# The front half of a transformer block on one core: instructions recorded, list-scheduled by the kernel itself, and held in that order on every engine

## The chip, the core and the metric

The kernel runs on one core of a Trainium2 chip. A core has five engines with a queue of instructions each: TensorE (PE in the profile; its weight loads are PEld), VectorE (DVE), ScalarE (ACT), GpSimd (POOL) and SyncE (SP, which issues most transfers). Each engine takes its instructions in the order in which they were emitted, and an instruction that has to wait holds up all that stand behind it on its engine. The metric is the device time of the whole program in microseconds: 648.29 before, the median of three runs (647.93, 648.29, 649.01).

## The reference

One block on 512 tokens of width 1024, all in float32:

```python
h = rmsnorm(x, attn_pre_g)
proj = h @ w_in                       # q, three kinds of k and v, gates
k_cmp, v_cmp = compress_kv(kc, ...), compress_kv(vc, ...)     # two small gelu MLPs
o_nsa = nsa_attention(...)            # 8 heads: compressed, selected and windowed keys, three gates
o_swa = swa_attention(...)            # 8 heads: window of 128, sinks
mix = concat([o_nsa, o_swa]) @ w_o
x = x + rmsnorm(mix, attn_post_g)
h = rmsnorm(x, mlp_pre_g)
a, u = split(h @ w_gate_up)           # 2 x 2816
y = (gelu(causal_dwconv(a)) * u) @ w_down
x = x + rmsnorm(y, mlp_post_g)
x = x + (p @ w_ple) * sigmoid(x @ w_ple_gate)
```

With 512 tokens all eight blocks of keys are selected, so the selected branch is causal attention over everything.

## The kernel before

**Arithmetic.** Every float32 operand is split in two float32r parts, `hi` (a rounded copy, on ACT) and `lo` (the rest, by a subtraction on DVE or POOL); a product is three matmuls, hi·hi, lo·hi and hi·lo. So each weight tile that is loaded costs an ACT copy and a subtraction before PE can use it (`weight`, lines 154 and 158), and each PE pass with 512 columns is one of some 680 such in the first half.

**The front half**, in the order in which it is written: `load_x` (x and the value weights arrive in eight chunks; per chunk the two parts of x, the two of the weight, and a square that is added up on DVE), `v_natural` (96 matmuls of 408 columns, lines 391 to 393), the compressed keys and values, the projections of k and the first three q, then `attention`. Attention is 8 units of NSA (2 groups of keys, 4 blocks of 128 queries) and 8 of the sliding window. A unit has two generators: the scores (PE into a PSUM tile named `pss`, the bias and the minimum on DVE at L675 or L637, the exponential on ACT at L682 or L642, the scaling by the sum on POOL at L580), and the products `pv` (four PE transposes into `pst`, L557; the hi part on ACT, L559, the lo part on DVE, L562; two matmuls into `pso`, L590). The scores of one unit are interleaved with the products of the unit before it.

**Fillers.** The remaining projections and the first part of the output projection are cut in steps of three matmuls (`fill_psmm`). After each step of attention `fill` hands out as many of them as a credit in nanoseconds allows, and `pin` ties each to an attention instruction a few steps back, so that it isn't moved ahead of it.

**Who orders.** The instructions are written in the order of these loops, but the order on each engine is set by the framework's list scheduler, which plays the program against its own timeline (`TCARGS = dict(schedule_with_timeline_sim=True)`) and emits what is ready first. Only what goes through `keep_in_program_order` stays in the order in which it was written.

**The end of the front half.** `out_proj` finishes the eight output tiles. Each is added to what was kept (DVE, L904), squared (ACT, L266 and L269), and the squares are added up, six times on POOL and the last time on DVE (L270). The sum goes through `rstd_col` (PE matmuls with a column of ones, L238; DVE L243; a power on POOL, L247) and `rstd_row` (PE transposes, L254). PE has 48 matmuls of the embedding product (`ple_tile`, PSUM tiles named `r_pss` and `r_psmm`) to do meanwhile: 18 stand ahead of the L238 matmuls, 18 between these and the transposes, 12 behind. Then the up-projection begins (L1551). The weights of its first four tiles (`upw`, held by `keep=True`) are split at the end of `out_proj`.

**Buffers.** PSUM tiles rotate per tag (`mm` 2, `s` 3, `t` 2, `o` 1); raw weights come through two slots (`wr`), and SP's next weight load waits until the older one has been split.

## Time and profile before

| | |
|---|---|
| median of 3 runs | 648.29 us |
| the profiled execution | 648.17 us, its span 646.4 us |
| granted TensorE clock | 1.00 in every stage |
| first real matmul (L391) | 5.50 us |
| first matmul after the output projection (`r_pss`) | 237.95 us |
| first matmul of the up-projection (L1551) | 250.68 us |
| busy over the span | PE 99%, DVE 79%, ACT 62%, POOL 26% |

A row of a timeline gives the start, the duration, the engine, the line, what is written from what is read, and in brackets how long the engine had been idle before and who ended that. PE's matmuls are pipelined: one of 512 columns is shown as lasting 0.39 us while the next one starts 0.23 us behind it, so the distance of two starts (the step) is what one costs, and a busy PE may still be waiting. In windows the columns are the stretch, its length, and for each engine the busy time and in brackets the number of instructions.

### The profile page before, as it was taken

The page shows a single profiled execution, that of the slowest core. Times are in us where ns is not written, and L with a number is a line of the kernel's source. Part 1 is how long each engine was busy: PE and PEld are TensorE (multiplying, and loading weights), DVE is VectorE, ACT ScalarE, POOL GpSimd, SP SyncE. Part 2 cuts the span into 40 slices and gives each one's busy share as a digit, 9 for nine tenths or more (in the row PEclk, how much of TensorE's full clock was granted, in tenths as well). Part 3 has the DMA queues.
Part 4 walks back from the last instruction along what each step waited for, and adds up shares of the span by engine and source line. Part 5 has one row for each costly group of instructions (what it writes and reads, how often), then busy time and mean ns, then how long its engine had stood idle before and what let it go on. Part 6 is the DMA issues. An engine that isn't in the chain of part 4 may idle for free.

```text
span 646.4 us, 11330 instructions
## 1 busy us (share of the span) xinstructions
PE 638.5 (99%) x4071; PEld 574.8 (89%) x4071; DVE 510.4 (79%) x1023; ACT 398.1 (62%) x759; POOL 166.2 (26%) x246
## 2 busy tenths in 40 slices
PE   8999999999999999999999999999999999999997
PEld 7988878878878887888999999999998999999986
DVE  7794787978766548799889889898999985756873
ACT  7554688878798658664676766767663443333351
POOL 1111588678487251111001010011100010201000
PEclk9999999999999999999999999999999999999999
DMA  8437720211245418386576755778754434377032
GB/s 307 161 109 206 212 67 21 64 48 51 82 139 220 163 33 299 113 239 149 124 190 151 202 150 137 204 172 254 181 149 143 133 98 126 116 252 264 2 115 81
DMA packets 45288, 95.78 MB, mean 148 GB/s; under 512 B 4400, under 2 KB 13744, under 8 KB 44976
## 3 DMA queue, kind: packets, MB, share of 16 engines
q1 hardware_dynamic: 40208, 84.49, 40.6%
q0 software_dynamic: 4880, 10.49, 9.8%
q8 instruction: 32, 0.52, 0.3%
q14 instruction: 24, 0.20, 0.1%
q10 hardware_dynamic: 144, 0.08, 0.1%
HBM read 81.41 MB, written 9.44 MB: 141 GB/s over the span
## 4 chain that ended last, share of the span: by engine, by line
PE 91%; DVE 3%; ACT 2%; DMA 1%; POOL 1%; issue 1%; SPq 0%; ACTq 0%; DVEq 0%
PE mlpup_psmm L175 7%; PE mlpup_psmm L179 7%; PE mlpup_psmm L178 7%; PE nsa_pso L590 2%; PE nsa_pst L557 2%; PE mlpdown_pst L175 2%; PE mlpdown_pst L178 2%; PE mlpdown_pst L179 2%; PE mlpup_pss L175 2%; PE mlpup_pss L179 2%; PE mlpup_pss L178 2%; PE mlpdown_pss L178 2%; PE mlpdown_pss L175 2%; PE mlpdown_pss L179 2%; PE mlpdown_psmm L175 1%; PE mlpup_pst L175 1%
## 5 line engine op out<-in xcount | busy, mean ns | idle before, releaser
L1168 POOL DMA_DIRECT2D mlpup_u<-in_gs_dram x17 | 20.9, 1230 | 155.4 <-DMA mlpup_u<-in_gs_dram 53.3
L179 PE MATMUL mlpup_psmm<-r_u,mlpup_wh 128*128 128x256 f32 x202 | 57.2, 283 | 0.0
L175 PE MATMUL mlpup_psmm<-r_u,mlpup_wh 128*128 128x256 f32 x202 | 57.1, 283 | 0.0
L178 PE MATMUL mlpup_psmm<-r_u,mlpup_wh 128*128 128x256 f32 x202 | 57.1, 283 | 0.0
L1260 ACT ACTIVATE mlpup_wh<-mlpup_u 128x1024 fp32r<-128x1024 f32 x37 | 39.2, 1060 | 25.3 <-PE mlpup_psmm L178 21.2
L154 ACT ACTIVATE mlpdown_wh<-mlpdown_wr 128x1024 fp32r<-128x1024 f32 (+1 forms) x24 | 23.7, 987 | 39.2 <-PE mlpdown_pst L178 10.3
L175 PE MATMUL mlpup_psmm<-mlpup_u,mlpup_wh 128*128 128x256 f32 (+1 forms) x158 | 47.0, 298 | 0.0
L179 PE MATMUL mlpup_psmm<-mlpup_u,mlpup_wh 128*128 128x256 f32 (+1 forms) x158 | 46.9, 297 | 0.0
L178 PE MATMUL mlpup_psmm<-mlpup_u,mlpup_wh 128*128 128x256 f32 (+1 forms) x158 | 46.9, 297 | 0.0
L1263 DVE TENSOR_TENSOR mlpup_wh<-mlpup_u,mlpup_wh 128x1024 fp32r<-128x1024 f32 x37 | 45.2, 1221 | 1.4 <-ACT mlpup_wh L1260 0.5
L580 POOL TENSOR_SCALAR nsa_u<-nsa_u,nsa_nrc,gate 128x512 f32<-128x512 f32 (+3 forms) x64 | 38.6, 615 | 14.7 <-DVE nsa_nrc L716 9.6
L682 ACT ACTIVATE nsa_u<-nsa_u,nsa_nnm 128x512 f32<-128x512 f32 (+3 forms) x64 | 35.4, 554 | 6.8 <-DVE nsa_nnm L675 6.6
L158 DVE TENSOR_TENSOR mlpdown_wh<-mlpdown_wr,mlpdown_wh 128x1024 fp32r<-128x1024 f32 (+1 forms) x24 | 27.8, 1157 | 14.8 <-ACT mlpdown_wh L154 14.6
L175 PEld LDWEIGHTS mlpup_psmm<-r_u,mlpup_wh 128*128 128x128 f32 x202 | 38.6, 191 | 0.0
L178 PEld LDWEIGHTS mlpup_psmm<-r_u,mlpup_wh 128*128 128x128 f32 x202 | 38.5, 191 | 0.0
L179 PEld LDWEIGHTS mlpup_psmm<-r_u,mlpup_wh 128*128 128x128 f32 x202 | 38.5, 191 | 0.0
L270 POOL TENSOR_TENSOR mlpdown_s<-mlpdown_s,mlpdown_s 128x512 f32<-128x512 f32 x6 | 9.3, 1552 | 105.5 <-ACT mlpdown_s L269 105.3
L1263 DVE TENSOR_TENSOR mlpup_wh<-mlpup_wr,mlpup_wh 128x1024 fp32r<-128x1024 f32 (+1 forms) x22 | 26.7, 1212 | 11.6 <-ACT mlpup_wh L1260 11.6
L562 DVE TENSOR_TENSOR nsa_u<-nsa_pst,nsa_u 128x512 fp32r<-128x512 f32 (+1 forms) x43 | 29.4, 686 | 6.8 <-ACT nsa_u L559 6.5
L158 POOL TENSOR_TENSOR fill_wh<-fill_wr,fill_wh 128x1024 fp32r<-128x1024 f32 (+2 forms) x13 | 24.5, 1887 | 26.5 <-ACT fill_wh L154 26.5
L175 PEld LDWEIGHTS mlpup_psmm<-mlpup_u,mlpup_wh 128*128 128x128 f32 x158 | 30.1, 191 | 0.9
L178 PEld LDWEIGHTS mlpup_psmm<-mlpup_u,mlpup_wh 128*128 128x128 f32 x158 | 30.1, 191 | 0.8
(537 smaller groups left out, 2346.7 us busy)
## 6 DMA issues: line engine op xcount, KB each, us to landing
mlpup_u<-in_gs_dram SPq DMA_DIRECT2D x34, 512.0 KB, 4.8
mlpup_u<-in_gs_dram POOLq DMA_DIRECT2D x17, 512.0 KB, 7.2
mlpup_wr<-in_gs_dram SPq DMA_DIRECT2D x17, 256.0 KB, 4.0
fill_wr<-in_win_dram SPq DMA_DIRECT2D x6, 512.0 KB, 3.7
fill_u<-fill_u SPq DMA_DIRECT2D x20, 128.0 KB, 2.7
mlpdown_wr<-in_down_dram SPq DMA_DIRECT2D x5, 512.0 KB, 3.9
loadx_u<-in_xT_dram SPq DMA_DIRECT2D x8, 256.0 KB, 4.9
compress_u<-projk_u SPq DMA_DIRECT2D x16, 128.0 KB, 2.4
```

The source lines that it names most:

```text
L154: h = nc.scalar.activation(hi, raw, AF.Copy)
L158: l = eng.tensor_sub(lw, raw, hi.bitcast(F32))
L175: r = self.pin(mm(ps, hi, x[:, 0, :], start=start, stop=False))
L178: mm(ps, lo, x[:, 0, :], start=False, stop=False)
L179: self.last = mm(ps, hi, x[:, 1, :], start=False, stop=stop).ins
L557: self.att(nc.tensor.transpose(pt[:, r * P : (r + 1) * P], src, self.ident))
L562: nc.vector.tensor_sub(t[rs, part, :], pt[rs], t[rs, 0, :].bitcast(F32))
L580: self.nc.gpsimd.tensor_scalar(ap, ap, col, gate, op0=ALU.mult, op1=ALU.mult)
L682: nc.scalar.activation(dst, dst, AF.Exp, bias=nm[:, r, b : b + 1], scale=-1.0, accum_out=sm[:, r, b : b + 1])
L1168: self.pin(self.nc.gpsimd.dma_start(o, a, accum_op=ALU.add, max_dma_last_dim=4 * ROWS))
L1260: return [nc.scalar.activation(w[key][0], src(), AF.Copy)]
L1263: return [nc.vector.tensor_sub(w[key][1], src(), w[key][0].bitcast(F32))]
```

## The change

A recording layer is put between the kernel and the engines. From the first load of x, calls to engines are not emitted but recorded as nodes, with the rectangles of the tiles that they read and write; the pools hand out stand-ins for tiles. When the last instruction of the output projection (with the splits of the first four up-projection weights) has been recorded, `play` makes one order for all engines: each time it takes the instruction that can start first by a table of costs per engine and shape (`cost`, with `MARGIN` 1.06 on all but PE), lags between engines, the number of buffers of each tag, the ACT table that is loaded, and a line of 240 bytes per ns for SP's transfers; of those that can start at once the one whose key (its own place in the recorded order, or that of an instruction that needs it, whichever is earlier) is lowest. SP's transfers are taken in the order of who needs them first. Then all are emitted in that order, each with `keep_in_program_order`. Pins are dropped for recorded instructions. What follows (the norm, the MLP, the down-projection) is emitted as before. Numbers of lines change: a recorded instruction shows the line of the helper, L376, and others L197.

```diff
+MARGIN = 1.06
+BEGIN = dict(PE=5.4, ACT=4.0, DVE=1.5, POOL=2.0, SP=0.8)
...
+class Recorder:
...
+    def schedule(self, live, begin):
+        lag = dict(PE=.25, ACT=.2, DVE=.2, POOL=.25, SP=.1)
...
+            x.key = min([x.n] + [y.n for y in x.after]) if x.engine != "SP" else min([y.n for y in x.after] or [x.n])
...
+        while len(done) < len(nodes):
+            best = None
+            for e, xs in ready.items():
+                xs.sort(key=lambda x: x.key)
+                some = xs[:1] if e == "SP" else xs[:60]
+                ts = [(start(x), x) for x in some]
+                ts = [(t, x) for t, x in ts if t is not None]
+                if ts:
+                    t = min(t for t, _ in ts)
+                    x = min((x for u, x in ts if u <= t + 1e-6), key=lambda x: x.key)
+                    if best is None or t < best[0]:
+                        best = (t, x)
...
+                x.end = clock[x.engine] = t + self.cost(x) * (1 if x.engine == "PE" else MARGIN)
...
+    def play(self, live, begin, hold):
+        self.on = False
+        for x in self.schedule(live, begin):
+            hold(x.call(*map(real, x.a), **{m: real(v) for m, v in x.k.items()}))
+        self.over = True
...
+    def hold(self, r):
+        return r if isinstance(r, Node) else self.tc.keep_in_program_order(r)
...
     def load_x(self):
         self.phase = "loadx"
         nc = self.nc
+        self.rec.on = True
...
+        live = [acc, *self.mo, *self.x1, *ple[0], *ple[2], *(t for w in ple[1] + self.upw for t in w)]
+        self.rec.play(live, BEGIN, self.hold)
         self.h2, self.f2 = [], []
         self.acc3 = self.norm_add(acc, "r2", C_GPOST, self.mo, self.x1, C_GMLP, self.h2, ple, 0)
```

Every engine has the same instructions in both programs. PE's last 2813 are in the same order, and so are DVE's last 487 and ACT's last 354: from the embedding product on, nothing is moved. Ahead of that the order differs on every engine. Three places:

PE, the products of the first NSA unit (`pst` are the transposes of probabilities, `pso` the matmuls with the values). Before:

```order
L557 MATMUL nsa_pst_1002<-ident,nsa_u_827 128x128
L557 MATMUL nsa_pst_1002<-ident,nsa_u_862 128x128
L557 MATMUL nsa_pst_1002<-ident,nsa_u_884 128x128
L557 MATMUL nsa_pst_1002<-ident,nsa_u_906 128x128
L590 MATMUL nsa_pso_955<-nsa_u_978,vnatural_u_338 128x512
L590 MATMUL nsa_pso_955<-nsa_u_994,vnatural_u_347 128x512
L557 MATMUL nsa_pst_1018<-ident,nsa_u_827 128x128
L557 MATMUL nsa_pst_1018<-ident,nsa_u_862 128x128
L557 MATMUL nsa_pst_1018<-ident,nsa_u_884 128x128
L557 MATMUL nsa_pst_1018<-ident,nsa_u_906 128x128
L590 MATMUL nsa_pso_955<-nsa_u_994,vnatural_u_347 128x512
L590 MATMUL nsa_pso_955<-nsa_u_1007,vnatural_u_356 128x512
```

and now:

```order
L376 MATMUL nsa_pso_1079<-nsa_u_1114,vnatural_u_460 128x512
L376 MATMUL nsa_pso_1079<-nsa_u_1138,vnatural_u_408 128x512
L376 MATMUL fill_psmm_1081<-loadx_u_170,fill_wh_837 128x512
L376 MATMUL fill_psmm_1081<-loadx_u_170,fill_wh_813 128x512
L376 MATMUL fill_psmm_1081<-loadx_u_200,fill_wh_813 128x512
L376 MATMUL nsa_pst_1159<-ident,nsa_u_833 128x128
L376 MATMUL nsa_pst_1159<-ident,nsa_u_855 128x128
L376 MATMUL nsa_pst_1159<-ident,nsa_u_869 128x128
L376 MATMUL nsa_pst_1159<-ident,nsa_u_929 128x128
L376 MATMUL nsa_pso_1079<-nsa_u_1138,vnatural_u_408 128x512
L376 MATMUL nsa_pso_1079<-nsa_u_1149,vnatural_u_432 128x512
```

Before, a group of transposes follows the pair of products at once; now one to three filler matmuls stand in many of these places. Ahead of the first `pso` there were 27 filler matmuls and are now 48 (18 of them ahead of the first score against windowed keys).

DVE, the end of the output projection (`outproj_wh` are subtractions for weights, `swa_u<-swa_u,outproj_ps` the additions of a finished tile, `outproj_s` the sum of squares). Before:

```order
L904 TENSOR_TENSOR swa_u_2228<-swa_u_2228,outproj_pss_2973 128x512
L904 TENSOR_TENSOR swa_u_2229<-swa_u_2229,outproj_psmm_2984 128x512
L904 TENSOR_TENSOR swa_u_2229<-swa_u_2229,outproj_pss_2995 128x512
L270 TENSOR_TENSOR outproj_s_2843<-outproj_s_2843,outproj_s_3003 128x512
L158 TENSOR_TENSOR outproj_wh_3007<-swa_u_2556,outproj_wh_3006 128x1024
L158 TENSOR_TENSOR outproj_wh_3011<-swa_u_2568,outproj_wh_3010 128x1024
L243 TENSOR_SCALAR r_rv_3055<-r_pst_3050 128x4
L158 TENSOR_TENSOR outproj_wh_3017<-outproj_wr_3014,outproj_wh_3016 128x1024
```

and now:

```order
L376 TENSOR_TENSOR swa_u_2684<-swa_u_2684,outproj_pss_2962 128x512
L376 TENSOR_TENSOR outproj_wh_2982<-swa_u_2866,outproj_wh_2966 128x1024
L376 TENSOR_TENSOR swa_u_2824<-swa_u_2824,outproj_psmm_2973 128x512
L376 TENSOR_TENSOR outproj_wh_2999<-swa_u_2871,outproj_wh_2991 128x1024
L376 TENSOR_TENSOR swa_u_2824<-swa_u_2824,outproj_pss_2988 128x512
L376 TENSOR_TENSOR outproj_wh_3007<-outproj_wr_2913,outproj_wh_3003 128x1024
L376 TENSOR_TENSOR outproj_s_2925<-outproj_s_2925,outproj_s_3009 128x512
L376 TENSOR_TENSOR outproj_wh_3014<-outproj_wr_2941,outproj_wh_3011 128x1024
L197 TENSOR_SCALAR r_rv_3047<-r_pst_3042 128x4
```

Three subtractions of 128x1024 now stand ahead of the last addition of squares, between the additions of the last tiles. On ACT the copies that feed them stand between the squares.

DVE, the start (`nsink` reads the columns of constants, `vc` and `compress_u` are cleared). Before:

```order
L330 TENSOR_SCALAR nsink<-cols 128x8
L367 CAST loadx_u_133<-loadx_u_106 128x408
L370 TENSOR_TENSOR loadx_u_134<-loadx_u_106,loadx_u_133 128x408
L371 SCALAR_TENSOR_TENSOR loadx_u_132<-loadx_u_104,cols,loadx_u_132 128x512
L370 TENSOR_TENSOR loadx_u_141<-loadx_u_109,loadx_u_140 128x408
```

and now:

```order
L376 MEMSET vc 128x256
L376 SCALAR_TENSOR_TENSOR loadx_u_152<-loadx_u_105,cols,loadx_u_152 128x512
L376 CAST loadx_u_165<-loadx_u_107 128x408
L376 TENSOR_TENSOR loadx_u_168<-loadx_u_107,loadx_u_165 128x408
L376 SCALAR_TENSOR_TENSOR loadx_u_170<-loadx_u_105,cols,loadx_u_170 128x512
```

The low part of the first chunk of x, which needs ACT's high part, now stands ahead of the cast of the first weight. On ACT, the tiny exponential that stood behind the second gelu now stands at the program's start, and the load of the exponential's table stands right ahead of the first exponential of attention.

More of the change, by code (lines that the diff above doesn't have):

```diff
@@ L342, in load_x @@
         acc = self.s([P, T])
-        keep = self.tc.keep_in_program_order
+        keep = self.hold
         raws = []
@@ L970, in norm_half @@
         nc = self.nc
-        keep = self.tc.keep_in_program_order
+        keep = self.hold
         ts = HALF[h]
@@ L1622, in mlp_down @@
         c = KC - 1
-        keep = self.tc.keep_in_program_order
+        keep = self.hold
         wts = []
```

257 lines of the change are left out of this document (243 added, 14 removed).

## The prediction

> **What bounds the kernel now.** I read the page first, then PE's timeline, then the windows of the front half, then the chain of waits.
>
> ```profile
> span 646.4 us, 11330 instructions
> PE 638.5 (99%) x4071; PEld 574.8 (89%) x4071; DVE 510.4 (79%) x1023; ACT 398.1 (62%) x759; POOL 166.2 (26%) x246
> PEclk9999999999999999999999999999999999999999
> PE 91%; DVE 3%; ACT 2%; DMA 1%; POOL 1%; issue 1%; SPq 0%; ACTq 0%; DVEq 0%
> ```
>
> PE is the bound: busy 99%, 91% of the chain, at full clock throughout. The change moves PE's matmuls but removes none, so all it can win are the gaps between them. Busy time hides these, so I take distances of starts:
>
> ```profile
> 7.06 0.34 PE L391 MATMUL vnatural_pso<-loadx_u,loadx_u 128*128 128x408 f32 x1
> 7.24 0.35 PE L392 MATMUL vnatural_pso<-loadx_u,loadx_u 128*128 128x408 f32 x1
> ...
> 69.64 0.39 PE L178 MATMUL projq_psmm<-loadx_u,projq_wh 128*128 128x512 f32 x1
> 69.87 0.39 PE L179 MATMUL projq_psmm<-loadx_u,projq_wh 128*128 128x512 f32 x1
> ...
> 80.16 0.28 PE L616 MATMUL nsa_pss<-compress_u,projq_u 128*128 128x256 f32 x1
> 80.27 0.28 PE L615 MATMUL nsa_pss<-compress_u,projq_u 128*128 128x256 f32 x1
> ...
> 86.05 0.60 PE L557 MATMUL nsa_pst<-ident,nsa_u 128*128 128x128 f32 x4
> 86.41 0.71 PE L590 MATMUL nsa_pso<-nsa_u,vnatural_u 128*128 128x512 f32 x2
> 86.95 0.60 PE L557 MATMUL nsa_pst<-ident,nsa_u 128*128 128x128 f32 x4
> ```
>
> A step without waiting is 0.227 us for 512 columns (median of all), 0.187 for 408, 0.119 for 256. Four transposes and two products take 86.95 - 86.05 = 0.90; less 2 x 0.227 that is 0.111 per transpose. The front half runs from the first to the last of these rows:
>
> ```profile
> 5.50 0.42 PE L391 MATMUL vnatural_pss<-loadx_u,loadx_u 128*128 128x408 f32 x1 [0.33 <-DVE loadx_u L367]
> 250.68 0.50 PE L1551 MATMUL mlpup_pss<-r_u,outproj_wh 128*128 128x512 f32 x1
> ```
>
> Between them stand 1302 records: 684 of 512 columns (155.3 us), 96 of 408 (18.0), 176 of 256 (21.0), 256 transposes (28.4), 64 of 288 to 416 (10.1 by 0.133 to 0.192), 26 small ones (2.2): 235.0 us of steps in 245.2 us. So 10.2 us are gaps, and this is the most that any order can win. Where they lie follows from the same sum by stretches of 20 us:
>
> ```profile
> 80.00:100.00 20.00, 19.42 (x110) 15.39 (x110) 17.03 (x78) 17.98 (x55) 16.64 (x29) 1.00 0.20 55
> 100.00:120.00 20.00, 19.90 (x117) 16.61 (x116) 15.68 (x58) 15.83 (x38) 14.35 (x23) 1.00 0.29 67
> 220.00:240.00 20.00, 20.00 (x89) 16.52 (x89) 9.69 (x14) 8.77 (x15) 8.96 (x7) 1.00 0.28 96
> ```
>
> From 80 to 100 the starts are 35 of 512 (7.9), 40 transposes (4.4), 14 of 256 (1.7) and 20 of 288 to 416 (3.5): 17.5 of 20.0 us, so 2.4 of gaps where PE is shown 97% busy. The eight stretches from 60 to 220 give 1.4, 2.4, 0.6, 1.4, 0.8, 1.1, 0.9 and 0.4: **9.0 us in attention**. The first chunk of x has 0.4, the stretch from 220 to 240 none, the norm 0.6. One such gap in the chain of waits:
>
> ```profile
> 84.48 0.37 POOL nsa_pc L711
> 84.85 1.73 POOL nsa_u L580 x4
> 86.58 0.73 POOL pw L727 x2
> 87.54 0.68 DVE nsa_u L562
> 88.27 0.66 PE nsa_pst L557 x4
> ```
>
> POOL scales, DVE splits a transposed block, and PE waits for it with nothing else at its head. ACT is busy 17.98, DVE 17.03 and POOL 16.64 of 20 us here: close to PE, but none of them full.
>
> **The change, part by part.** *Attention.* Work is equal; PE gets a filler matmul (0.227 us) where a group of transposes would follow a product at once. It is worth between 0 (the gaps only move) and 9.0 us (none is left). Where fillers already alternate with attention the trace has 0.6 (100 to 120) and 0.4 (200 to 220) per 20 us; where products follow one another without fillers it has 2.4. The new order resembles the former nearly everywhere: 48 filler matmuls instead of 27 ahead of the first product, and one to three in most gaps after it. Eight stretches at 0.4 to 0.6 leave 3.3 to 5.0; I take 3.5 left, **-5.5 us**. The range for what is left is 1.5 to 6.
>
> *The start.* These rows set when PE begins:
>
> ```profile
> 4.61 0.72 ACT L365 ACTIVATE loadx_u<-loadx_u,cols 128x512 fp32r<-128x512 f32 x1 [1.89 <-DMA cols<-in_cols_dram]
> 4.98 0.37 DVE L367 CAST loadx_u<-loadx_u 128x408 fp32r<-128x408 f32 x1 [0.20 <-DMA loadx_u<-in_wv_dram]
> 5.89 0.75 DVE L371 SCALAR_TENSOR_TENSOR loadx_u<-loadx_u,cols,loadx_u 128x512 fp32r<-128x512 f32 x1
> 6.03 0.46 PE L392 MATMUL vnatural_pss<-loadx_u,loadx_u 128*128 128x408 f32 x1
> ```
>
> Now the 0.75 us operation stands ahead of the cast and waits for ACT (4.61 + 0.72 = 5.33). It ends near 6.05, the cast near 6.4, and PE starts near 6.45 instead of 5.50. Three products need only the cast (0.56 us), in which the low part of the weight (0.58) gets nearly done. Twelve matmuls then end near 8.73 (6.45 + 12 x 0.187 + 0.04), where before, with a gap of 0.43 behind the first one, they ended at 8.17. **+0.6 us**, between 0.3 and 0.9. From the second chunk on DVE needs some 1.9 us per chunk and PE 12 x 0.187 = 2.24, so nothing more is lost, and nothing catches up either.
>
> *The end of the output projection.* Here the order loses, by a contention that the cost table doesn't know. Two pairs of rows show it:
>
> ```profile
> 61.39 2.40 POOL L158 TENSOR_TENSOR fill_wh<-fill_wr,fill_wh 128x1024 fp32r<-128x1024 f32 x1 [17.40 <-ACT fill_wh L154]
> 61.86 2.48 DVE L426 TENSOR_TENSOR projq_u<-projq_s,projq_u 128x512 fp32r<-128x512 f32 x1 [2.51 <-ACT projq_u L424]
> ```
>
> ```profile
> 232.18 1.22 DVE L158 TENSOR_TENSOR outproj_wh<-outproj_wr,outproj_wh 128x1024 fp32r<-128x1024 f32 x1
> 241.48 0.69 DVE L270 TENSOR_TENSOR outproj_s<-outproj_s,outproj_s 128x512 f32<-128x512 f32 x1 [2.64 <-POOL outproj_s L270]
> L270 POOL TENSOR_TENSOR outproj_s<-outproj_s,outproj_s x6: 1292/1304/2342, 232.2 to 240.2; 128x512 f32<-128x512 f32 x6
> 237.95 0.40 PE L175 MATMUL r_pss<-pletiles_u,pletiles_wh 128*128 128x512 f32 x1
> 242.22 1.05 PE L238 MATMUL r_pst<-ones,outproj_s 128*128 128x1 f32 x8
> ```
>
> The DVE subtraction of 512 usually takes 0.68 us; started inside POOL's subtraction (61.39 to 63.79) it lasts until 64.34. The first POOL addition, started at 232.21 inside DVE's subtraction (until 233.40), lasts 2.34 instead of 1.30. Whichever starts second waits for the first, and then still needs 0.55 to 1.15. Additions on DVE that read PSUM (L904) aren't slowed. Let X be the start of the first `r_pss` (237.95 before). Before, the chain of POOL additions ended at X + 3.5, DVE's last one at X + 4.2, and L238 began at X + 4.27, right behind its 18 matmuls (18 x 0.23 = 4.15). Now the output tiles end at 6-matmul steps of 1.36 us before X, and the subtraction of weight 2982 meets the fourth POOL addition (X - 2.15 to X - 0.85): DVE is busy until X + 0.3, POOL's fifth waits and ends at X + 1.45, DVE's addition of tile 7 slips from X - 1.16 to X + 1.0, subtraction 2999 waits for POOL until X + 1.45 and ends at X + 2.6, POOL's sixth addition ends at X + 3.75, the addition of tile 8 at X + 3.3, subtraction 3007 waits until X + 3.75 and ends at X + 4.9, and only then comes the last addition of squares, to X + 5.6. L238 begins near X + 5.65 instead of X + 4.27: **+1.4 us**. From below it is 0 (the operations don't meet), from above 2.5 (each of the three subtractions costs POOL a whole 1.22 on the chain, less the 1 us that a shorter chain gives). The 18 matmuls between L238 and the transposes (4.1 us) cover the power on POOL (1.96 at most in this trace), so it doesn't grow.
>
> *The exponential's table.*
>
> ```profile
> 58.86 1.28 ACT L527 ACT_TABLE_LOAD   x1
> 60.16 0.20 ACT L527 ACTIVATE compressout_act<-ones 128x1 f32<-128x1 f32 x1
> ```
>
> It moves from behind the second gelu to the head of the first exponential and costs ACT 60.16 - 58.86 = 1.30 us there. Between the first two score tiles and the first windowed ones PE now has 18 fillers, 4.1 us: I cost it at nothing, and at 1.3 if that cover is gone. With the cover gone the sum below would be -2.2 instead of -3.5. The Trainium skill ("ScalarE: Activation LUTs", What ACT_TABLE_LOAD costs) speaks more strongly against such a move: 1283 ns for the load and 1380 ns of drain, 2.66 us for each switch, with which the sum without cover would be -0.8. The rows agree with the load and show no drain behind it, so I keep theirs.
>
> **Sum.** -5.5 + 0.6 + 1.4 = -3.5 us, from the first matmul on; everything behind L1551 keeps its order and PE has no gaps to speak of there. The profiled execution took 648.17 us (span 646.4 and 1.8 around it), 0.1 below the median of 648.29. **648.2 - 3.5 = 644.7 us.** Its own range: -7.5 + 0.3 + 0 to -3.0 + 0.9 + 2.5, 641.0 to 648.6.
>
> **The rivals.**
>
> *The gaps of attention vanish and the end doesn't slip.* For it: the stretch from 220 to 240 has no gap at all once nothing of attention is waited for, and all four engines have idle time left in each stretch above. Against it: the rows of the contention at the end. -8.5 + 0.6: 640.3 us.
>
> *The gaps only move.* ACT is at 90% and DVE at 85% in the first products; more fillers early mean fewer later, since all 264 are used anyway. If 7 of 9.0 us come back, the two losses are as large as the gain: 648.2 - 2.0 + 0.6 + 1.4 = 648.2 us.
>
> *A load holds up SP's queue* (slower). In one order for all engines a weight load whose slot isn't free keeps the moves behind it waiting, and these carry q and k:
>
> ```profile
> SPq L166 <- POOL fill_wh L158: 51.9, 7, 15.3
> ```
>
> SP waited for POOL to split a weight 7 times, 15.3 us at worst. The place is the load of a filler weight right ahead of the eight moves of the windowed keys: PE has 18 fillers (4.1 us) to bridge it, so it decides from a wait of 4.1 us on. At 15.3 PE loses 11.2: 644.7 + 11.2, about 656 us; at 8 us it is 648.6. Against it: the slot that this load takes is freed by a DVE subtraction that stands eight rows ahead of the one that makes these keys, so it should have been free for long.
>
> **How the numbers follow.** A difference under 0.2% (1.3 us) can't be told from none: faster is below 647.0, slower above 649.6. The forecast gets 0.58, the clean order 0.15, moved gaps 0.14, the held queue 0.13. Faster: 0.55 of the forecast's 0.58, 0.15 of the clean order, 0.03 of the moved gaps, 0.73. Same: 0.03 and 0.08, 0.11. Slower: 0.03 and 0.13, 0.16. The range reaches to the clean order at one end and over the moved gaps at the other, 640.2 to 649.0, and leaves out the slow rival.
>
> **What would show it.** Step sums from 60 to 220 that leave 1.5 to 6 us of gaps; the first matmul near 6.4 us; DVE subtractions of 1024 elements that last over 1.5 us beside POOL additions, and L238 more than 5 us behind the first `r_pss`, with a gap of over 0.5 us ahead of it. It would be wrong if PE waited on a DMA or on scores in the first NSA unit, if the losses at start and end were absent, or if the MLP changed by more than 0.5 us.

## The result: 0.6% slower

| | median us | runs, range |
|---|---|---|
| before | 648.62 | 4, 647.93 to 649.01 |
| after | 652.55 | 4, 652.22 to 652.90 |
| after, second series | 650.30 | 5, 648.94 to 652.10 |
| before, beside the second series | 648.54 | 28, 647.73 to 649.65 and one of 1267.84 |

Ratio after to before: 1.0062, 95% interval 1.0044 to 1.0079; in the second series 1.0036, 1.0022 to 1.0049. The forecast was 644.7 us, range 640.2 to 649.0. It was wrong in sign. The first profiled execution of the changed kernel took 652.84 us (span 651.1, 4.7 over the span before), the second 648.94 us (span 647.2, 0.8 over it). That one kernel gives both is the first thing to explain. The one execution of before of 1267.84 us and one of 1614.32 us of the kernel with start and end mended stand far outside all others and are left out of the ratios.

The page of the first profile, its rows that answer to those shown of before:

```profile
span 651.1 us, 11311 instructions
PE 640.6 (98%) x4071; PEld 578.2 (89%) x4071; DVE 511.8 (79%) x1023; ACT 396.9 (61%) x759; POOL 165.6 (25%) x246
PEclk9999999999999998999999999999999999999999
PE 91%; DVE 4%; ACT 2%; DMA 1%; issue 1%; DVEq 0%; SPq 0%
```

Still PE's kernel, but one slice of PEclk shows an 8. PE's timeline of the same profile (start, busy us, what it waited for) has the places where time was lost:

```profile
6.39 3.40 PE L376 MATMUL vnatural_pss<-loadx_u,loadx_u 128*128 128x408 f32 x9 [0.67 <-ACT loadx_u L376]
...
38.84 0.47 PE L376 MATMUL projk_psmm<-loadx_u,projk_wh 128*128 128x512 f32 x1 [0.17 <-DVE compress_s L376]
39.63 0.33 PE L376 MATMUL compress_pss<-compress_wh,compress_u 128*66 128x256 f32 x1 [0.33 <-ACT compress_u L376]
40.55 5.51 PE L376 MATMUL projk_psmm<-loadx_u,projk_wh 128*128 128x512 f32 x23 [0.59 <-DVE projk_wh L376]
...
245.29 1.02 PE L197 MATMUL r_pst<-ones,outproj_s 128*128 128x1 f32 x8 [1.01 <-DVE outproj_s L376]
246.18 2.85 PE L197 MATMUL r_psmm<-pletiles_u,pletiles_wh 128*128 128x512 f32 x6
```

The same stretches in the second profile of the same kernel, first the start, then the part behind L238 (which begins at 242.95 there):

```profile
6.78 1.90 PE L376 MATMUL vnatural_pss<-loadx_u,loadx_u 128*128 128x408 f32 x9 [1.54 <-ACT loadx_u L376]
```

Nine products of 408 columns take 1.90 us there and 3.40 in the first profile, where their starts are 0.340 us apart instead of 0.187. Behind L238 six products of 512 take 2.85 us (0.427 apart) in the first profile; in the second they step at 0.23. The granted clock says the same. Windows of the first profile (PEclk is the third number from the end):

```profile
244.00:246.00 2.00, 0.98 (x9) 0.74 (x7) 2.00 (x3) 1.53 (x3) 0.00 (x0) 1.00 0.22 78
246.00:248.00 2.00, 2.00 (x8) 1.62 (x9) 0.44 (x2) 0.00 (x0) 1.04 (x1) 0.56 0.84 254
248.00:250.00 2.00, 2.00 (x7) 1.58 (x6) 0.00 (x0) 0.60 (x1) 0.00 (x0) 0.58 0.80 287
```

In the trace's records of the clock the first profile has it full from 10.73 us on and halved from 246.25 to 249.66; the second has it full from 4.54 us and never halved before the program's last microseconds; before had it full from 4.38.

By the prediction's own method (differences of the stage marks, and step sums for the gaps), against the profile of before:

| part of the program | forecast | first profile | second profile |
|---|---|---|---|
| last matmul of the first product (before: 23.52; 26.03; 24.43) | +0.6 | +2.51 | +0.91 |
| gaps from 20 to 60 us (0.34; 2.44; 2.44) | 0 | +2.10 | +2.10 |
| gaps from 60 to 222 us (9.00; 6.37; 5.62) | -5.5 | -2.63 | -3.38 |
| first `r_pss` to L238 (4.27; 5.35; 5.36) | +1.4 | +1.08 | +1.09 |
| L238 to the first product of the MLP (8.46; 10.00; 8.46) | 0 | +1.54 | 0 |
| sum | -3.5 | +4.6 | +0.7 |

The spans differ by +4.7 and +0.8: the table holds all but 0.1 us of it. The MLP keeps its time (395.8 us from its first product to the end in all three).

### The profile page after: what moved, and what is told of

Its sections match the earlier page's. It is cut to its first block, busy times and chain, and to the rows that moved or that the text cites. A ratio compares the mean times of both kernels' runs of the same rounds, so it can differ in the third digit from the quotient of the medians.

```text
span 651.1 us, 11311 instructions
## 1 busy us (share of the span) xinstructions
PE 640.6 (98%) x4071; PEld 578.2 (89%) x4071; DVE 511.8 (79%) x1023; ACT 396.9 (61%) x759; POOL 165.6 (25%) x246
## 4 chain that ended last, share of the span: by engine, by line
PE 91%; DVE 4%; ACT 2%; DMA 1%; issue 1%; DVEq 0%; SPq 0%
PE mlpup_psmm L197 23%; PE fill_psmm L376 8%; PE mlpup_pss L197 8%; PE mlpdown_pst L197 6%; PE mlpup_pst L197 5%; PE mlpdown_pss L197 5%; PE mlpdown_psmm L197 4%; PE norm_pss L197 3%; PE nsa_pso L376 3%; PE projq_psmm L376 3%; PE nsa_pst L376 3%; PE nsa_pss L376 2%; PE vnatural_pss L376 2%; PE mlpup_pso L197 2%; PE projk_psmm L376 2%; PE swa_pso L376 1%
## 5 line engine op out<-in xcount | busy, mean ns | idle before, releaser
L197 PE MATMUL mlpup_psmm<-r_u,mlpup_wh 128*128 128x256 f32 (+1 forms) x612 | 79.5, 283 | 0.1
L197 PEld LDWEIGHTS mlpup_psmm<-r_u,mlpup_wh 128*128 128x128 f32 x612 | 76.1, 191 | 0.6 <-DVE mlpup_wh L197 0.4
L197 PE MATMUL mlpup_psmm<-mlpup_u,mlpup_wh 128*128 128x256 f32 (+1 forms) x474 | 69.4, 297 | 0.0
L197 PEld LDWEIGHTS mlpup_psmm<-mlpup_u,mlpup_wh 128*128 128x128 f32 x474 | 63.5, 190 | 2.6
L197 POOL DMA_DIRECT2D mlpup_u<-in_gs_dram x17 | 20.9, 1230 | 155.8 <-DMA mlpup_u<-in_gs_dram 41.2
L197 ACT ACTIVATE mlpup_wh<-mlpup_u 128x1024 fp32r<-128x1024 f32 x37 | 39.2, 1060 | 25.6 <-PE mlpup_psmm L197 21.5
L197 ACT ACTIVATE mlpdown_wh<-mlpdown_wr 128x1024 fp32r<-128x1024 f32 (+1 forms) x24 | 23.7, 988 | 40.3 <-PE mlpdown_pst L197 10.9
L197 DVE TENSOR_TENSOR mlpup_wh<-mlpup_u,mlpup_wh 128x1024 fp32r<-128x1024 f32 x37 | 45.2, 1220 | 1.5 <-ACT mlpup_wh L197 0.5
L376 PE MATMUL fill_psmm<-loadx_u,fill_wh 128*128 128x512 f32 x144 | 45.1, 403 | 0.0
L197 PE MATMUL mlpdown_pst<-mlpup_u,mlpdown_wh 128*128 128x512 f32 (+1 forms) x228 | 44.9, 340 | 0.0
L376 POOL TENSOR_SCALAR nsa_u<-nsa_u,nsa_nrc,gate 128x512 f32<-128x512 f32 (+3 forms) x64 | 38.5, 612 | 12.4 <-DVE nsa_nrc L376 10.1
L197 PEld LDWEIGHTS mlpdown_pst<-mlpup_u,mlpdown_wh 128*128 128x128 f32 x228 | 37.0, 189 | 4.9
L197 DVE TENSOR_TENSOR mlpdown_wh<-mlpdown_wr,mlpdown_wh 128x1024 fp32r<-128x1024 f32 (+1 forms) x24 | 27.2, 1135 | 17.7 <-ACT mlpdown_wh L197 17.6
L376 ACT ACTIVATE nsa_u<-nsa_u,nsa_nnm 128x512 f32<-128x512 f32 (+3 forms) x64 | 35.3, 555 | 5.9 <-DVE nsa_nnm L376 4.6
L197 DVE TENSOR_TENSOR mlpup_wh<-mlpup_wr,mlpup_wh 128x1024 fp32r<-128x1024 f32 (+1 forms) x23 | 27.9, 1212 | 11.8 <-ACT mlpup_wh L197 11.8
L197 POOL TENSOR_TENSOR mlpdown_s<-mlpdown_s,mlpdown_s 128x512 f32<-128x512 f32 x6 | 9.5, 1578 | 106.3 <-ACT mlpdown_s L197 106.1
L197 PE MATMUL mlpdown_pss<-mlpup_u,mlpdown_wh 128*128 128x256 f32 x246 | 35.8, 282 | 0.0
L376 POOL TENSOR_TENSOR fill_wh<-fill_wr,fill_wh 128x1024 fp32r<-128x1024 f32 (+2 forms) x13 | 24.5, 1889 | 33.9 <-DVE compress_u L376 22.2
L197 PEld LDWEIGHTS mlpdown_pss<-mlpup_u,mlpdown_wh 128*128 128x128 f32 x246 | 32.5, 191 | 0.3
L376 DVE TENSOR_TENSOR nsa_u<-nsa_pst,nsa_u 128x512 fp32r<-128x512 f32 (+1 forms) x43 | 28.6, 685 | 4.5 <-ACT nsa_u L376 4.0
L376 DVE CUSTOM_DVE_ANT_0 nsa_u<-nsa_pss,biastables_u 128x128 f32<-128x128 f32 (+4 forms) x64 | 27.3, 446 | 5.0 <-PE nsa_pss L376 2.8
L197 PE MATMUL mlpdown_psmm<-mlpup_u,mlpdown_wh 128*128 128x256 f32 (+1 forms) x180 | 31.1, 320 | 0.0
```

What stands on the lines that cost most here:

```text
L197: return f(*map(real, a), **{m: real(x) for m, x in k.items()})
L376: hold(x.call(*map(real, x.a), **{m: real(v) for m, v in x.k.items()}))
```

## Experiments

Fourteen kernels ran, each timed in alternation with the kernel before. Most edits give the planner artificial dependencies or other prices, so they change the order and nothing that is computed. "After" is the unedited changed kernel.

| kernel | median us | ratio to before, 95% interval |
|---|---|---|
| end mended | 647.61 | 0.9989 (0.9976 to 1.0002) |
| start mended | 648.74 | 1.0010 (0.9999 to 1.0020) |
| DVE's order behind the first product | 657.78 | 1.0143 (1.0129 to 1.0157) |
| these three together | 648.44 | 1.0002 (0.9993 to 1.0011) |
| after, again | 650.30 | 1.0036 (1.0022 to 1.0049) |
| start and end mended | 646.84 | 0.9977 (0.9968 to 0.9986) |
| four tiles ahead of L238 | 649.16 | 1.0005 (0.9994 to 1.0017) |
| 11 warm-ups | 650.22 | 1.0024 (1.0015 to 1.0033) |
| start, end, price of the exponential | 644.07 | 0.9934 (0.9922 to 0.9946) |
| the same, three prices on DVE | 645.13 | 0.9943 (0.9930 to 0.9956) |
| start, end, exponential; two operations kept apart | 644.02 | 0.9922 (0.9908 to 0.9936) |
| start, end, exponential; loads at 360 GB/s | 646.23 | 0.9969 (0.9955 to 0.9983) |
| the same, projk's split back to its old place | 645.52 | 0.9938 (0.9919 to 0.9957) |
| price of the exponential alone | 647.28 | 0.9970 (0.9958 to 0.9982) |

### The end mended

```diff
             if c == KC - 1:
+                n0 = len(self.rec.nodes)
                 self.upw = [...]
+                for x in self.rec.nodes[n0:]:
+                    if x.engine in ("DVE", "ACT"):
+                        x.deps.add(self.rec.nodes[n0 - 1])
```

> Only the end is mended: the planner is told that the splits of the last four weights (ACT casts, DVE subtractions of 1024) come behind the last addition of squares. Theory (lock, then clock): the 1.19 us gap ahead of L238 goes, L238 begins about 4.2 to 4.4 us behind the first r_pss instead of 5.35, and the nine matmuls behind it, which step at 0.427 us in the changed kernel, step at 0.227, some 1.9 us more. 652.5 - 1.1 - 1.9 = 649.5 us. Rival (the half-speed stretch isn't caused by the gap, and comes in any case behind the eight 1-column matmuls): the gap goes but the stretch stays, 651.4 us. Rival (the splits are only shifted, and the MLP then waits for its first weights): 652 us or more, with PE waiting for mlpup weights near 255 us.

647.61 us. DVE in the unedited kernel's first profile, then in this one:

```profile
238.03 2.02 DVE L376 TENSOR_TENSOR outproj_wh<-swa_u,outproj_wh 128x1024 fp32r<-128x1024 f32 x1
...
240.57 1.72 DVE L376 TENSOR_TENSOR outproj_wh<-swa_u,outproj_wh 128x1024 fp32r<-128x1024 f32 x1
...
242.81 1.73 DVE L376 TENSOR_TENSOR outproj_wh<-outproj_wr,outproj_wh 128x1024 fp32r<-128x1024 f32 x1
244.47 0.68 DVE L376 TENSOR_TENSOR outproj_s<-outproj_s,outproj_s 128x512 f32<-128x512 f32 x1
```

```profile
239.22 0.69 DVE L376 TENSOR_TENSOR outproj_s<-outproj_s,outproj_s 128x512 f32<-128x512 f32 x1 [0.87 <-POOL outproj_s L376]
240.06 2.36 DVE L376 TENSOR_TENSOR outproj_wh<-swa_u,outproj_wh 128x1024 fp32r<-128x1024 f32 x2
```

The subtractions take 2.02, 1.72 and 1.73 us between POOL's additions, and 1.2 each (2.36 for two) behind them. L238 begins 4.17 us behind the first `r_pss` (241.63 and 237.46) instead of 5.35, and the products behind it step at 0.23. So the blocking of the prediction (POOL and DVE lengthen each other's operations) is real and costs about what it said. The time fell by more than the 1.1 and 1.9 us expected. Part of it was not the edit: in this profile the clock is full from 5.88 us, although the start is that of the unedited kernel.

### The start mended

```diff
         self.xacc = acc
+        for e in ("ACT", "DVE"):
+            xs = [x for x in self.rec.nodes if x.engine == e]
+            for a, b in zip(xs, xs[1:]):
+                b.deps.add(a)
```

> Only the start is mended: on ACT and DVE the operations of the loads of x are held in the order of recording, so the cast of the first weight comes ahead of the low part of x, as in the kernel before. Part of the order behind it is drawn up anew by that. Theory (the late start costs clock too): first matmul near 5.5 us instead of 6.39 (-0.9), and the eleven steps of 0.340 us become 0.187 (-1.7): 652.5 - 2.6 = 649.9 us. Rival (when the clock rises hangs on the launch and not on the gap): -0.9 only, 651.6 us, and the half-speed steps last to the same time, some 10.7 us. Rival (the 0.9 is lost later, since the loads of x pace the first product): 652.5 us.

648.74 us. The first product begins at 5.52 us, and the clock is full from 6.37. Why the planner had it otherwise is 0.06 us: by its prices the low part of x can start at 4.91 us and the first weight is there at 4.96. Of the end, 1.18 us of gap ahead of L238 stays, but the clock doesn't fall behind it in this profile.

### DVE's order behind the first product, and all three

```diff
+        for x in self.later:
+            x.deps.update(y for y in self.rec.nodes[n0:] if y.engine == "DVE" and y.name in ("tensor_mul", "tensor_copy"))
```

`self.later` holds DVE's operations for the gate of the first v tile and all of those for the other three.

> Only DVE's order behind the first product is changed: the row of r1 and the four evictions of the first compressed projection come ahead of the splits and gates of the last three v tiles (in the changed kernel they come behind all four). Theory: PE's gaps of 0.33, 0.56, 0.80 and 0.36 us between 38 and 50 us come from DVE, which gets to these evictions at 36.2 us; they go, and PE's later work moves up by 2.05 us: 650.5 us. Rival (they come back as waits for the first attention scores, since the chain on DVE, ACT and POOL sets when these begin): 652.5 us, with the gaps at 79 to 89 us grown from 1.96 to some 4 us.

657.78 us, 4.9 us above the slowest run of after: a miss for both theories. PE's waits from 30 to 60 us:

```profile
PE projk_psmm L376 <- DVE projk_wh L376: 6.8, 1, 6.8
```

Moving the evictions forward left the split of the projk weight behind everything that was put off: DVE did it at 44.46 us, 5.2 later than in the unedited kernel (39.28). So DVE's order in this stretch does decide; the edit picked the wrong operation.

> The three edits together. Theory (three independent terms): 652.5 - 3.0 - 2.6 - 2.0 = 644.9 us, which is the gain in attention alone and near the forecast of 644.7. Rival (the clock terms don't go): 644.9 + 3.6 = 648.5 us. Rival (the gaps at the start of attention grow by what is won ahead of them): 647 us or more, PE's gaps from 75 to 100 us at 4 us or more by step sums instead of 2.85.

648.44 us: the three don't add up, since the third edit cost 3.2 us of gaps (1.89 at 44.2, 1.31 at 47.1) here too. It is dropped below.

### The unedited kernel again, and start and end mended

> The changed kernel itself, unedited, in more executions and with a second profile, beside the three kernels below. Theory (when TensorE's rate rises at the start and whether it falls at the end hangs on where a free-running window of some 3.4 us lies against the idle stretches): the times spread over some 4 us, from about 648.8 (the gaps alone: 647.6 of the kernel with the mended end, and 1.2) to 652.9, and the second profile has half-speed steps at other places than the first. Rival (the half-speed stretches belong to this order and come each time): 652.2 to 652.9 us again, with steps of 0.340 us until 10.7 and of 0.427 us from 246.2 to 249.7 us.

648.94 to 652.10 us, median 650.30: it spreads over 3.2 us, and its profile is the second one above. The half-speed stretches don't belong to the order as such. Seven of the nine executions of after have a mean granted clock of 0.996 or 0.997, like the first profile; two have 0.999, like the second. One of these took 652.25 us all the same. A late rise of the clock at the start, which this mean doesn't count, would explain 1.6 us of its distance to 648.94; the other 1.7 us stay open.

> The mended end and the mended start together, without the edit of DVE's order behind the first product, which made things worse. Theory (the terms add): the kernel with the mended start has 1.18 us of gap ahead of L238 left, without it 648.74 - 1.2 = 647.5 us, at most 0.5 less where the rate had fallen behind that gap in some executions: 647.0 to 647.5. Rival (the mended end brought 4.9 us of itself): 643.9 to 645 us. Rival (no better than the mended end alone): 647.6 us.

646.84 us, 0.23% faster than before (interval 0.14% to 0.32%): the forecast sign, with two local mends. The start adds 0.8 us to the gain of the end, by the two medians.

### Covering the gap at the end; bridging the one at the start

```diff
-        for i in range(3):
+        for i in range(4):
             self.ple_tile(ple, i)
         y = self.rstd_col(acc, cname)
-        for i in range(3, 6):
+        for i in range(4, 6):
```

> The changed kernel with one of the eight gate tiles behind the output projection (6 matmuls, 1.38 us) moved from behind L238 to ahead of it: four tiles ahead instead of three, two behind. DVE and POOL keep their order, so they go on blocking one another (DVE subtractions of 1.7 to 2.0 us), but PE has work while they do. Theory (the gap costs by PE's idleness, and the clock by that too): no gap of over 0.3 us ahead of L238, no steps of 0.427 us behind it, and the same time as the kernel with the mended end, 647.6 us, within 0.6. Rival (the half-speed stretch comes from the eight 1-column matmuls or from DVE's and POOL's load): the gap goes, the stretch stays, and the time is 1.2 below that of the unedited kernel.

DVE's and PE's timelines of this kernel:

```profile
237.46 2.01 DVE L376 TENSOR_TENSOR outproj_wh<-swa_u,outproj_wh 128x1024 fp32r<-128x1024 f32 x1
...
242.23 1.73 DVE L376 TENSOR_TENSOR outproj_wh<-outproj_wr,outproj_wh 128x1024 fp32r<-128x1024 f32 x1
```

```profile
243.54 1.55 PE L197 MATMUL r_psmm<-pletiles_u,pletiles_wh 128*128 128x512 f32 x6
244.93 0.95 PE L197 MATMUL r_pst<-ones,outproj_s 128*128 128x1 f32 x8
245.74 1.64 PE L197 MATMUL r_pss<-pletiles_u,pletiles_wh 128*128 128x512 f32 x6
```

DVE and POOL block one another as before, PE has no gap, and the clock stays: in this profile the eight 1-column matmuls and the blocking alone don't lower it. The lowest time is that of the mended end (647.38 and 647.31); the median is 1.5 us higher, 649.16. Its times lie in two groups, 647.4 to 648.2 and 648.9 to 650.4, and its profile is of the second: half speed until 10.83 us, at a start that is the same as in the kernel with the mended end. With one profile it is not shown that the clock at the start makes the two groups.

> The changed kernel with 11 instead of 9 warm-up matmuls, so that PE idles for less than 0.1 us instead of 0.9 ahead of its first product at about 6.4 us. Nothing else is changed. Theory (idling keeps TensorE at half its rate for one more window): the rate rises at 8 us at the latest in every profile, and the median is 0.5 to 1.7 us below that of the unedited kernel. Rival (the launch alone sets when the rate rises): the median is that of the unedited kernel, within 0.4 us.

650.22 us, no better than after. The two more warm-ups ran at 0.427 us each. In its profile the clock is full from 7.66 us, but the first product began at 6.74, where the first profile of after has 6.39 and the second 6.78. The warm-ups had ended at 6.38, and PE then waited for the operands of the first chunk, on which ACT began when the constants had landed (at 4.81 us; 4.46 and 4.84 in after). So the later start isn't shown to come from the warm-ups, and the run doesn't settle what they are worth.

### One price: the exponential

`cost` takes the size of an operation from its first output and its first input. In the first half of attention the exponentials write over their input and sum into a column, the column counts as the first output, another column (the minimum) as the first input, and 0.29 us is planned for each of the 64. The trace of after, ACT's groups from 75 to 140 us (busy, mean ns of one):

```profile
L376 ACT ACTIVATE nsa_u<-nsa_u,nsa_nnm 128x512 f32<-128x512 f32 x16 | 11.5, 718 | 4.8 <-DVE nsa_nnm L376 4.6
L376 ACT ACTIVATION_READ_ACCUMULATOR nsa_u<-nsa_u,nsa_nnm 128x1 f32 x43 | 8.1, 188 | 0.0
L376 ACT ACTIVATE nsa_u<-nsa_u,nsa_nnm 128x384 f32<-128x384 f32 x8 | 4.8, 607 | 1.0 <-DVE nsa_nrc L376 1.0
...
L376 ACT ACTIVATE nsa_u<-nsa_u,nsa_nnm 128x128 f32<-128x128 f32 x11 | 4.3, 391 | 0.0
...
L376 ACT ACTIVATE nsa_u<-nsa_u,nsa_nnm 128x256 f32<-128x256 f32 x8 | 4.0, 501 | 0.1
```

So they take 0.39 to 0.72 us, and the reading of the sum lies partly beside the next one. Over all of ACT's recorded work the plan has 153.8 us where the trace has 168.1 (these are the 14 us of the expectation below: more work, not lateness). While the plan of after foresaw 0.6 us of PE gaps behind the first chunk of x, its operations on POOL ran 6.5 us late at 79 us of the plan, 10.5 at 131 and 11.0 at 190: behind the start and the compression, the slip builds up where these exponentials are densest.

```diff
         if e == "ACT":
+            n = max(int(np.prod(v.shape[1:])) for v in node.writes + node.reads)
             t = (.07 if psum else .1) + .00083 * n
```

> The kernel with mended start and end, and one price of the planner put right: an exponential that writes over its own input and sums into a column (64 of them on ACT in the first half of attention) is priced by its 128 to 512 columns (0.40 to 0.74 us) instead of by the one column of its sum (0.29 us whatever its size). The trace of the changed kernel has 0.40, 0.51 and 0.62 us for 128, 256 and 384 columns. Theory (the gain in attention fell short because ACT ran 14 us behind its plan there): by step sums PE's gaps from 75 to 140 us fall from some 5.1 us to under 3, and the time by 2 us, to about 644.8 us median. Rival (the plan has no slack on ACT, DVE and POOL that better prices could use): gaps and time within 0.5 us of 646.8. Rival (another order in attention costs as much elsewhere, by chance): 647.5 us or more.

644.07 us, 0.66% faster than before (0.54% to 0.78%) and 2.8 us below the same kernel without the price. Windows of that one, then of this one:

```profile
75.00:100.00 25.00, 23.55 (x130) 19.45 (x129) 16.86 (x81) 17.79 (x50) 17.43 (x31) 1.00 0.44 102
100.00:140.00 40.00, 39.36 (x228) 32.34 (x228) 34.17 (x134) 33.34 (x88) 31.45 (x46) 1.00 0.20 54
```

```profile
75.00:100.00 25.00, 23.21 (x131) 19.50 (x129) 16.66 (x81) 18.03 (x50) 17.42 (x31) 1.00 0.45 104
100.00:140.00 40.00, 40.00 (x240) 34.38 (x239) 36.01 (x148) 34.90 (x97) 33.51 (x50) 1.00 0.25 67
```

From 100 to 140 us PE gets 240 matmuls into the time of 228. By step sums the gaps from 75 to 140 fall from 5.1 to 3.2 us, a little less than expected. What is left from 75 to 100 are two waits of 0.87 and 1.25 us ahead of the first scores, the longer one for a DMA of the keys.

> The same, and three prices on DVE put to what the trace has: reciprocals 0.10 to 0.22 us instead of 0.08 to 0.10, small additions 0.17 instead of 0.09, the evictions on 64 partitions 0.615 instead of 0.49. With them the plan itself foresees 3.3 us of PE gaps (1.0 from 20 to 40, 0.6 from 40 to 60, 1.8 from 160 to 180 us), where without them it foresaw none. Theory (the gaps from 20 to 60 us come from these prices): measured gaps there fall from 2.2 to about the 1.5 of the plan, and the new gap near 170 us costs 1.8: 1.1 us above the kernel before it in this list, some 645.9 us. Rival (DVE's and POOL's blocking one another, which no price holds, makes the gaps from 20 to 60): they stay at 2 us or more, and the time is 1.8 above the kernel before it, or more.

645.13 us. The gap that the plan foresaw near 170 us came (1.3 us at 177 to 179). The gaps from 20 to 60 us stayed at 2.2 (2.4 without these prices): these three prices alone aren't their cause.

> The changed kernel with the price of the exponential put right and nothing else: start and end are those of the changed kernel. Theory (that price is what the gain in attention lacked): by step sums PE's gaps from 60 to 222 us are 3.5 us or less, where the changed kernel has 5.6 and 6.4 in its two profiles, and the median is 2 to 3 us below its 650.3: 647.3 to 648.3 us. Rival (the gain came only together with the mended start): 5.5 us of gaps or more, and 650 us.

647.28 us, 3.0 below the second series of after. The gaps from 60 to 222 us are 2.8 us: with the price right, the forecast of 3.5 left in attention is reached and passed, with nothing else changed. That this isn't a lucky order is borne out by the other profiles: the nine without the price have about 5.4 to 6.5 us there, the six with it 2.8 to 4.4, but for one of 7.0 in which PE waits 3.3 us for a DMA (below). The end is that of after, and in this profile the clock fell behind it:

```profile
239.75 1.02 PE L197 MATMUL r_pst<-ones,outproj_s 128*128 128x1 f32 x8 [1.00 <-DVE outproj_s L377]
240.63 2.26 PE L197 MATMUL r_psmm<-pletiles_u,pletiles_wh 128*128 128x512 f32 x6
```

One wait that is left in attention comes from blocking. PE's gap of 0.85 us ahead of the scores at 79.37 us ends with DVE's minimum (`nsa_nmp`), and DVE gets to this late, because its subtraction for the keys lies inside POOL's split of a filler weight. The first profile of after:

```profile
75.86 2.40 POOL L376 TENSOR_TENSOR fill_wh<-fill_wr,fill_wh 128x1024 fp32r<-128x1024 f32 x1 [9.23 <-ACT fill_wh L376]
76.70 2.10 DVE L376 TENSOR_TENSOR projk_u<-projk_s,projk_u 128x512 fp32r<-128x512 f32 x1
79.37 0.50 PE L376 MATMUL nsa_pss<-compress_u,projq_u 128*128 128x288 f32 x2 [0.69 <-DVE nsa_nmp L376]
```

In the kernel before, this subtraction takes 0.69 us. In the twelve profiles of changed kernels in which it takes 2.10, PE has the gap, 0.84 to 0.88 us; in the three in which it takes 0.69 (three prices on DVE, and the two with loads at 360 GB/s below), it hasn't. No run changed this alone.

### The gaps from 20 to 60 us

Before has only 0.34 us of them, with DVE nearly full. Its window:

```profile
30.00:40.00 10.00, 10.00 (x48) 8.29 (x47) 9.55 (x22) 3.61 (x6) 0.77 (x2) 1.00 0.52 207
```

> The kernel with mended start and end and the price of the exponential put right, and two operations kept apart behind the first product: the second DVE subtraction of 1024 waits for POOL's power (in that kernel the power takes 1.9 us beside it, 1.02 alone), and POOL's three selections for the bias tables wait for DVE's second split of the compressed keys (DVE's first one takes 1.11 us beside them, 0.70 alone). Theory (DVE's and POOL's blocking makes the gaps from 20 to 60 us): the first eviction on DVE comes 0.9 us earlier against PE and the split of the projk weight by 1.3, PE's gap ahead of projk (1.1 us) goes, the gaps from 20 to 60 us fall from 2.4 to about 1 us, 642.8 us median. Rival (prices and blocking each make about half, and the chain on DVE has no slack): they fall by 0.5 to 0.9 us, 643.4 us. Rival (DVE's own load sets it): no change, 644.1 us.

```diff
+        subs[0].deps.update(x for x in self.rec.nodes if x.engine == "POOL" and x.name == "tensor_tensor")
...
+            if x.name == "affine_select":
+                x.deps.add(subs[-1])
```

644.02 us, the same, and it tells nothing on blocking: POOL's power still took 1.93 us, the plan moved POOL's selections from 33 to 40 us, but the chip ran them at 36.11, where they had stood, since no data made them wait and POOL had nothing ahead of them:

```profile
36.11 2.75 POOL L377 TENSOR_SCALAR_AFFINE_SELECT biastables_u<-biastables_u 128x512 f32<-128x512 f32 x3 [5.48 <-DVE biastables_u L377]
```

The order is held on each engine, not between engines; an artificial dependency only moves an operation that has something to stand behind.

> The kernel with mended start and end and the price of the exponential put right, and one number more: the planner counts a load at 360 GB/s instead of 240 (the trace has 350 to 430 GB/s whenever several loads are under way ahead of 40 us). With 240 it believes that the second weight of the compressed keys is there at 23 us, when it is split from 20.4 to 22.1; so on DVE the second subtraction of 1024 stands behind the small operation of the norm, which waits for PE until 24.2, and then runs beside POOL's power, which takes 1.9 us instead of 1.02, while DVE was idle for 1.7 us ahead of it. Theory (a late plan of the loads makes about half of the gaps from 20 to 60 us): DVE subtracts at about 22.1, the power takes 1.02 us, DVE's chain behind it comes 0.9 us earlier, PE's gaps of 0.25 (at 26.7) and 1.13 us (at 37.4) fall to under 0.5 together, and the median is 643.2 us. Rival (DVE's small operations and evictions, priced too low, set it): gaps and time within 0.3 us of that kernel, 644.1 us. Rival (another order in attention costs as much by chance): 645 us.

```diff
-                wire = max(wire, t + 1.8) + size / 240e3
+                wire = max(wire, t + 1.8) + size / 360e3
```

646.23 us. The step that it was for came true: the second subtraction moved ahead of the norm, and POOL's power took 1.02 us instead of 1.93:

```profile
25.51 1.02 POOL L377 TENSOR_TENSOR r1c<-vnatural_rv,mhalf 128x4 f32<-128x4 f32 x1 [21.19 <-DVE vnatural_rv L377]
```

The wait ahead of projk didn't shrink (1.28 us; 1.13 without the edit). So this blocking costs 0.9 us on POOL and, in this order, nothing that PE shows ahead of projk. Why the median is 2.2 us higher stays open: the times spread from 644.18 to 649.06 us, and the profiled one, of 644.95, is as fast as that of the kernel without the edit (645.04). A wait of 1.25 us for the keys' DMA stands in both profiles.

> The kernel before this in the list (loads counted at 360 GB/s), with one part of the change undone: the split of the projk weight (ACT's cast, DVE's subtraction of 1024) stands ahead of the four v tiles again, as in the kernel before, where DVE did it from 26.0 to 27.2 us, inside the time in which it waits for the norm anyway. PE's order is the same up to the first scores. Theory (DVE's order makes PE's gaps from 20 to 60 us, by a weight that is split too late): the wait of 1.28 us ahead of projk at 38.1 goes, what is left from 20 to 60 us is under 1.2 us (2.26 without it), and the time falls by 1.1 us, to 645.1 us, if the gap at the first scores (1.25 us, on a DMA of the keys) doesn't grow; to 646.2 if it takes the gain. Rival (DVE's load as a whole sets it): the gaps move to the products of the compression but their sum stays within 0.4 us.

```diff
+        self.norm[0].deps.add(next(x for x in self.rec.nodes[n0:] if x.name == "tensor_sub"))
...
+        w9 = self.proj_weight(9)
+        hi, lo = self.rec.nodes[-2:]
+        for x in self.vn + self.norm[1:]:
+            x.deps.add(hi if x.engine == "ACT" else lo)
```

The first line keeps the second subtraction of the compressed keys' weight ahead of the norm, where the kernel before this has it. DVE in after, where the split of the projk weight begins at 39.28, and here:

```profile
30.75 0.69 DVE L376 COPY r1b<-vnatural_pst 128x512 f32<-128x512 f32 x1 [1.25 <-PE vnatural_pst L376]
...
36.23 2.46 DVE L376 TENSOR_TENSOR compress_s<-compress_psmm,r1b 64x256 f32<-64x256 f32 x4
...
39.28 1.22 DVE L376 TENSOR_TENSOR projk_wh<-projk_wr,projk_wh 128x1024 fp32r<-128x1024 f32 x1
```

```profile
26.41 1.23 DVE L377 TENSOR_TENSOR projk_wh<-projk_wr,projk_wh 128x1024 fp32r<-128x1024 f32 x1 [1.26 <-ACT projk_wh L377]
```

With the split back in a stretch in which DVE waits for the norm, the wait ahead of projk is gone and the gaps from 20 to 60 us fall from 2.26 to 1.30 us. That shows the place of this split in DVE's order to be the cause of 1.0 us of the gaps in this kernel, where after has 2.1 us more than before; 0.64 us (a later weight of the compression) and small gaps are left, and whether DVE's load or its blocking with POOL makes these stays open. The median fell by 0.7 us only, to 645.52, which the spread of both series (643.20 to 647.14 here) hardly tells from none. The profiled execution, the slowest of the six, has a longer wait for the keys. PE's longest wait from 20 to 100 us, and the clock behind it:

```profile
PE nsa_pss L377 <- DMA compress_u<-projk_u: 3.3, 1, 3.3
```

```profile
78.00:80.00 2.00, 2.00 (x7) 1.70 (x6) 1.37 (x7) 1.86 (x6) 0.12 (x1) 0.50 1.08 268
```

This wait differs between executions of one kernel: the first profile of after has 0.59 us of it, the second none. So it is not shown that the edit made it grow.

## Why the prediction was wrong, step by step

- **Attention, -5.5: the right mechanism, mis-sized.** -2.63 and -3.38 in the two profiles; 6.4 and 5.6 us were left, where I had taken 3.5 in a range of 1.5 to 6. I took it from stretches of the old kernel where fillers already alternated, and didn't ask whether the plan knew the engines that feed PE. It priced ACT's exponentials at about half. With that price mended alone, 2.8 us are left. And 0.85 us of what was left is the contention that the prediction priced at the end only: DVE's subtraction of 2.10 us beside POOL's.
- **"It would be wrong if PE waited on a DMA or on scores in the first NSA unit": it did both.** In the first profile 0.85 and 0.52 us at 79 and 88 us for DVE's work on scores, and 0.59 us at 83 us for a DMA of the keys; in the second only the two for DVE.
- **From the start of the compression to 60 us, forecast at nothing: +2.10 in both profiles.** This step is missing from the sum. The prediction followed moved instructions at the two ends and in attention, and not DVE's order between 24 and 46 us, where DVE is nearly full before (9.55 of 10 us from 30 to 40). The split of the projk weight, moved out of a stretch in which DVE waited, came out again ahead of PE: 1.0 us by the run that put it back. What makes the rest is open.
- **The start, +0.6: right as a delay, incomplete as a price.** First product at 6.39 (forecast 6.45); +0.91 when the clock is up in time. When it isn't, 1.6 us more. The prediction reckoned the twelve products behind it at 0.187 us each.
- **The end, +1.4: right, by the mechanism and nearly the size.** +1.08; subtractions of 2.02, 1.72 and 1.73 us, L238 at +5.35 (forecast 5.65). What it left out is that the gap can cost the clock of the 3.41 us behind it: +1.54 in the first profile.
- **The table load at nothing:** right; no wait of PE from 60 to 100 us is put down to ACT, and soon behind its first exponential ACT itself waits 0.98 us for DVE.
- **The rivals.** "The gaps only move" said 7 us of gaps, nearest to the 6.4 and 5.6 measured, but its reason, that ACT and DVE are too full and the fillers run out, doesn't hold: with the price mended 2.8 us are left with the same fillers. The held SP queue wasn't what made the kernel slower: PE waited for the keys' moves 0.59 us in one profile and not at all in the other. In the kernels mended further that wait was up to 3.3 us.
- **The chances.** 0.73 on faster put too much on one number, the gaps that a plan leaves, which no row of before bounds.

So in the second profile, without clock losses, after is 0.7 us slower than before: the start, the stretch to 60 us and the end (0.91 + 2.10 + 1.09) take more than attention gains (3.38). In the first, with clock losses of 1.6 and 1.5 us, and less gained in attention, it is 4.6 us slower.

## What to carry to other kernels

A list-scheduled order is as good as its prices: compare the plan's begin times with the trace's on each engine, and mend the first price at which the slip grows (here one line, 3 us). The old order hid a weight split in an idle moment of an engine off the critical path; a new order must be read there too, where an engine is nearly full, and not only at its ends. Here a gap on PE of about 1 us cost up to 2.7: the clock fell behind it or rose one window later.

## What the runs showed of the hardware

TensorE's clock moved in steps of one window: 3.41 us from halving to full in three kernels (246.25 to 249.66, 241.39 to 244.81, 77.69 to 81.11), and two windows around the wait of 6.8 us in the kernel with DVE's order changed (44.27 to 51.10). Counted from the first rise in windows of 3.413 us, these halvings fall on a boundary to within 0.1 us, some 236 us later in two of them. So it is a grid, and where it lies against the program differs from execution to execution: the first rise came at 10.73 and 4.54 us in after's two profiles, 1.81 windows apart. In thirteen profiles the clock was full from a time between 4.4 and 7.7 us on, in three from 10.1 to 10.8.

- In those three (10.73, 10.83, 10.14) the clock did not rise at the end of the window that ended 3.41 us earlier, which held 0.87, 0.89 and 1.20 us without a matmul between the warm-ups and the first product. No window that ended in a rise held more than 0.54 us (before, ahead of its first warm-up at 1.51 us).
- Behind the gap at L238 the clock fell in the two profiles whose window held all of the gap and all of the eight 1-column matmuls, 2.06 us of 3.41. It stayed where the window held 1.83 us of both (0.94 and 0.89), 1.80, 1.71 and 1.31.

How little idleness was needed I had not expected. The Trainium skill ("TensorE: Matmul & The Clock Gate", Part 1: The HAM clock gate) has the free-running window of 3413 ns, which the trace agrees with, and gives a window of idleness as what brings the half rate; here about 60% of one was enough, if 1-column matmuls count as idle.

DVE and POOL blocking one another showed at three more places: POOL's power 1.93 us beside a DVE subtraction of 1024 (kernels with the start mended; 1.02 alone), DVE's split of 528 columns 1.11 us beside POOL's selections (0.70 alone), and POOL's fifth and sixth additions of squares 2.17 and 1.95 us (1.30 alone).
